# Conditioning weights of the first norm: multiplied on TensorE in column quarters instead of folded on VectorE

## The chip, the cores and the metric

The kernel runs on one core of a Trainium2 chip. The metric is the device time of one launch in microseconds (us). TensorE (PE in the profile; PEld is its weight load) multiplies, VectorE (DVE) and ScalarE (ACT) do elementwise work and reductions, GpSimd (POOL) does almost nothing here, and SyncE (SP) issues every DMA from one queue, in program order. Each engine runs its own instructions in order and waits for others by semaphores.

## The reference, cut to what matters

A two-layer trunk for 256 tokens of width 2048: in each layer a mixer and an MLP, each behind a norm whose shift and scale come from a conditioning vector `c`.

```python
cond = jax.nn.silu(c)                                  # [2048]
for l in range(2):
    mod = cond @ ada_w[l] + ada_b[l]                   # [2048] @ [2048, 6*2048]
    sh1, sc1, g1, sh2, sc2, g2 = split(mod, 6)
    h = rms_norm(x, norm1_g[l]) * (1 + sc1) + sh1      # the change is in this sh1, sc1 of l = 0
    y = mixer(h)
    x = x + g1 * y
    h = rms_norm(x, norm2_g[l]) * (1 + sc2) + sh2
    x = x + g2 * square(relu(h @ mlp_w1[l])) @ mlp_w2[l]
```

Nothing of the first layer can be multiplied before `sh1` and `sc1` of its columns are known: they need 2 x 2048 columns of `ada_w[0]`, 2048 rows each, or 64 DMAs of 512 KB.

## The kernel before, in words

Activations are held feature-major: a k-tile is 128 features by 256 tokens, and there are 16. Shift and scale of two k-tiles are made together, as a *pair* `pr` (0 to 7). For a pair, `load_ar` brings 4 tiles `ar`, each with 4 row blocks of `ada_w` by 512 columns (256 of shift, 256 of scale), in two DMAs; the ring has 4 such tiles, so the whole ring is one pair. `cond_sum` multiplies the 16 row blocks by their column of `cond` and adds them up on VectorE (L575 once, L577 15 times) into `acc`, 128 partitions by 512. `cond_pair` then sums over the partitions: `row_sums` transposes `acc` in four pieces (L317), ScalarE adds up each row (L320), and two small VectorE instructions give shift and scale (L588, L590), with which ScalarE makes the normed input `hf` of the two k-tiles (L595).

Around this the first products are laid out so that they can begin with few k-tiles. I call them phase 1 (k-tiles 0 to 3: values of six heads and first queries, `nb` and `q0b`, weights loaded in L624), phase 2 (k-tiles 0 to 7: gates and last values, `gbs` and `vbs`, weights from `wplain`, L607) and phase 3 (all k-tiles: other queries and keys, `qk`). In phase 3 the k-tiles 0 to 5 are multiplied as plain f32 (`hf` by `raw`), and from k-tile 6 on the weights are split into a high part (`wh`, ScalarE, L224) and a low part (`wl`, VectorE, L225). All these matmuls are issued by the helper `mm`, L124. The pairs 0 and 1 stand in phase 1, the sums of 2 and 3 with the first loads of phase 2, those of 4 and 5 in its second half, 6 and 7 in phase 3. `gates()` stands at k-tile 8 of phase 3 and needs all 16 k-tiles.

The eight banks of PSUM are handed out as four of `lin` (L) and four of `mix` (M0 to M3). In the three phases only M3 is free for the conditioning work. The order of each engine's instructions is set by a scheduler at build time, from the order of the code and its own estimates; it isn't changed at run time.

Of the kernel before, what the change touches and what calls it, by code (L numbers as in the profile page):

```python
# [9 lines left out]
F32 = mybir.dt.float32  # L10
# [3 lines left out]
OP = mybir.AluOpType  # L14
# [4 lines left out]
P = 128  # L19
# [7 lines left out]

# [1 line left out]
_C0 = {"ident": 128, "ones": 128}  # L29
# [58 lines left out]
def back(ap):  # L88
    """The same elements, last first along the free axis."""
    a = [list(s) for s in ap.ap]  # L90
    return bass.AP(tensor=ap.tensor, offset=ap.offset + a[1][1] - 1, ap=[a[0], [-1, a[1][1]]])
# [3 lines left out]
def tile_trunk(ctx: ExitStack, tc: tile.TileContext, io, out):  # L95
# [23 lines left out]
    def sums(n):  # L119
        """n banks for long sums: the four of `lin`, then the first of `mix`."""  # L120
        return [lbank() if i < 4 else bank(i - 4) for i in range(n)]
# [3 lines left out]

# [1 line left out]
    c0o, c0w = _cuts(_C0)  # L127
# [46 lines left out]

# [1 line left out]
    def newton(y, v, a):  # L176
        """y, near v ** -0.5, one step nearer."""
        V.tensor_tensor(a, y, y, op=OP.mult)
        V.scalar_tensor_tensor(a, a, -0.5, v, op0=OP.mult, op1=OP.mult)
        V.scalar_tensor_tensor(y, a, 1.5, y, op0=OP.add, op1=OP.mult)  # L180
# [11 lines left out]
    def spread(cols, which=None):  # L192
        """[128 tokens, 2] columns -> [128, 256] with the token on the free axis, on each partition."""
        dg = tmp.tile([P, T], F32, tag="diag", bufs=2, name="diag")
        for t in range(2):
            V.tensor_scalar(dg[:, t * P:(t + 1) * P], ident, cols[:, t:t + 1], None, op0=OP.mult)
        b = bank(which)
        mm(b[:, 0:T], ones, dg)
        return b[:, 0:T]
# [12 lines left out]
    def side():  # L212
        """The next of the small steps that go between the long products."""
        if pending:
            f = pending.pop(0)
            if f is not None:
                f()

# [1 line left out]
    def wsplit(raw, n):  # L220
# [7 lines left out]
    def wload(W, k0, kper, cols):  # L228
        """k-tiles k0.. of the column ranges `cols`, side by side, as exact high and low parts."""
        w = sum(c1 - c0_ for c0_, c1 in cols)  # L230
        raw = wp.tile([P, 1024], F32, tag="raw", bufs=4, name="raw")
        rv = raw[:, :kper * w].rearrange("p (k c) -> p k c", k=kper)
        o = 0
        for a, b in cols:
            SP.dma_start(rv[:, :, o:o + b - a],  # L235
                         W[k0 * P:(k0 + kper) * P, a:b].rearrange("(k p) c -> p k c", p=P))
            o += b - a
        return wsplit(raw, kper * w)

    def tmul(o, h, wh, wl, c, m, start, stop):  # L240
        """o[:, :256] + o[:, 256:] += W[:, c:c+m]^T h, feature-major."""
        mm(o[0:m, 0:2 * T], wh[:, c:c + m], h[:, 0:2 * T], start=start, stop=False)
        mm(o[0:m, 0:T], wl[:, c:c + m], h[:, 0:T], start=False, stop=stop)

    def linear(W, nk, kper, cols, hget, plan, evac, banks, stag=1, fill=None, k1=0):
        """Feature-major products. plan: one entry per bank, of one tile (offset in the W tile, width), whose
        product is the sum of the bank's halves, or of two tiles, one in each half."""
        w = sum(b - a for a, b in cols)
# [35 lines left out]
    def linear_n(W, nk, kper, c0_, hget, evac, fill=None, k1=0):  # L284
        """Token-major products of 512 columns."""
        bs = [lbank() for _ in range(2)]
        for k0 in range(k1, nk, kper):
            wh, wl = wload(W, k0, kper, [(c0_, c0_ + 512)])
            if fill is not None:
                fill()  # L290
            for t in range(2):
                for kk in range(kper):
                    k = k0 + kk
                    nmul(bs[t], hget(k), t, wh[:, kk * 512:(kk + 1) * 512], wl[:, kk * 512:(kk + 1) * 512],
                         k == k1, k == nk - 1)
                side()
        for t in range(2):
            evac(t, bs[t])
# [12 lines left out]

# [1 line left out]
    def row_sums(dst, tiles, func=AF.Copy, which=None):  # L313
        """dst[:, i] = the sum over the partitions of each column of func(tiles[i])."""
        b = bank(which)
        for i, t in enumerate(tiles):
            PE.transpose(b[:, i * P:(i + 1) * P], t, ident)  # L317
        for i in range(len(tiles)):
            j = tmp.tile([P, P], F32, tag="junk", bufs=2, name="junk")
            S.activation(j, b[:, i * P:(i + 1) * P], func, accum_out=dst[:, i:i + 1])  # L320
# [40 lines left out]
    class Fill:  # L361
        """Spreads the conditioning products over the weight tiles of a phase."""

# [21 lines left out]

# [1 line left out]
    class Norm:  # L387
# [43 lines left out]
    def residual(W, nk, hget, gate, norm, groups, stag, fill, done=None):  # L431
        """xT += gate * (W^T h); groups: the plans of output tiles that are held together, and their banks."""
        k0 = 0
# [56 lines left out]

# [1 line left out]
    wE = io["even_w_in"][0]  # L492
# [8 lines left out]
    def vtile():  # L501
        """Values of two heads, each with a column of ones behind."""
        v = vp.tile([P, 2, 2, 260], F32, tag="v", name="v")
# [10 lines left out]
    with ExitStack() as es:  # L514
# [9 lines left out]
        for t in range(2):  # L524
            for q in range(2):
                SP.dma_start(xn[t][q], x[t * P:(t + 1) * P, q * 1024:(q + 1) * 1024])
            if t == 0:
                SP.dma_start(c0, io["c0"])
                r0, n0 = load_rows(0)

        def load_ar(pr, kq):
            ar = sp0.tile([P, 4, 2, T], F32, tag="ar", bufs=4, name="ar")
# [8 lines left out]
        put_rows(0, r0, n0)  # L541
        S.activation(cond, prm[:, 96:112], AF.Silu)
        for i in (1, 2):
            put_rows(i, *rows[i - 1])
# [22 lines left out]
        def cond_sum(pr):  # L567
            """The products for the k-tiles 2 pr and 2 pr + 1, still to be summed over the partitions."""
            acc = sums_of[pr] = sp0.tile([P, 2, T], F32, tag="acc0", bufs=3, name="acc0")
            for kq in range(4):  # L570
                ar = early.pop(0) if early else load_ar(pr, kq)
                for kr in range(4):
                    cc = cond[:, kq * 4 + kr:kq * 4 + kr + 1]
                    if kq == 0 and kr == 0:
                        V.tensor_scalar(acc, ar[:, kr], cc, None, op0=OP.mult)  # L575
                    else:
                        V.scalar_tensor_tensor(acc, ar[:, kr], cc, acc, op0=OP.mult, op1=OP.add)  # L577

        def cond_pair(pr):
            """Shift, scale and the normed input of the k-tiles 2 pr and 2 pr + 1."""  # L580
            if pr not in sums_of:
                cond_sum(pr)
            acc = sums_of.pop(pr)
            cs = st(4, "adac")
            row_sums(cs, [acc[:, i // 2, (i % 2) * P:(i % 2 + 1) * P] for i in range(4)])
            two_k = slice(2 * pr, 2 * pr + 2)
# [12 lines left out]

        # The values of the first six heads and the first queries, over a quarter of the k-tiles, as these come.  # L600
        HALF = KT // 2
# [36 lines left out]

        # The gates of the first four heads and the values of the last two, over half of the k-tiles.
        gbs = [lbank() for _ in range(4)]  # L640
# [39 lines left out]
        def gates():  # L680
            """Weights of the scores of the first four heads, and the floors of their denominators."""
            gb = small.tile([8, 1], F32, tag="gb", bufs=1, name="gb")
# [57 lines left out]

        # The other queries and all keys of the first half of the heads, over all k-tiles.
        qk = sums(7)
# [25 lines left out]

# [1 line left out]
    mp = mixs.enter_context(tc.tile_pool(name="mp", bufs=1))  # L770
# [7 lines left out]
    def mix_head(hd, qt, kt, v, gate, weight, ml):  # L778
        """One head: masked, weighted scores, values, head norm, gate. v(t): the head's values of a token tile."""
        x_ = {}  # L780
# [125 lines left out]
    def segment(*units, k1=0):  # L906
        """256 feature-major columns for each (first column, what to do with their bank)."""
        n = len(units)
# [25 lines left out]

    # The rest of the first products.
    nb = sums(6)
# [64 lines left out]

# [1 line left out]
    fill = Fill([(1, 2)], 60)  # L1003
    hs = nrm.finish(1, 0)
    wO = io["odd_w_in"][0]
    with ExitStack() as es:
# [82 lines left out]

        # top 64 of the causal keys, as an additive mask  # L1090
        m8 = ap.tile([P, 8], F32, name="m8")
# [96 lines left out]

# [1 line left out]
    ready = set()  # L1190
# [47 lines left out]
```

## Time and profile before

| | |
|---|---|
| median of 3 runs | 2418.57 us (2410.31 to 2423.73) |
| profiled execution, span | 2418.6 us |
| TensorE, mean granted clock | 0.988 |
| busy: PE, DVE, ACT | 96%, 72%, 50% of the span |
| HBM read | 607.37 MB |

The profiled execution's span and the median of the runs agree within 0.1 us, so a sum made on the trace can be read against the median. A record's time includes the tail in which its result comes out, so that in a dense stream the next record starts before the last has ended; how fast matmuls go is read from the distance of their starts, or from the chain's rows, which give the time from the first start to the next piece.

### The profile page before, as it was taken

What the parts mean: (1) busy time and instruction counts of PE and PEld (TensorE: products, weight loads), DVE (VectorE), ACT (ScalarE), POOL (GpSimd) and SP (SyncE); (2) the same over time, 40 slices, a digit from 0 to 9 for tenths busy, and PEclk for the clock granted to TensorE, in tenths of its full rate; (3) what the DMA queues carried; (4) which work ended last, traced back from release to release, by engine and by line L of the source; (5) the groups of instructions that cost most, each with busy time, mean ns of one, the idle gap of its engine ahead of it and who ended that gap; (6) DMA issues with size and microseconds to landing.
All of it is one profiled execution on the core that took longest, in us unless ns stands there. A gap on an engine that the chain in (4) does not pass through costs nothing.

```text
span 2418.6 us, 38953 instructions
## 1 busy us (share of the span) xinstructions
PE 2331.7 (96%) x14877; PEld 2091.8 (86%) x14877; DVE 1737.4 (72%) x2555; ACT 1209.8 (50%) x2293; POOL 0.5 (0%) x8
## 2 busy tenths in 40 slices
PE   5899999999899999999999899999999999999999
PEld 3688889998788888899899799998888888999998
DVE  5768899987877777887877879886555546556554
ACT  2235554544555555655544445655555556444443
POOL 0000000000000000000000000000000000000000
PEclk9999999999899999999999999999999999999999
DMA  9998899988788898888888776675666666555653
GB/s 324 358 297 292 284 302 320 328 283 288 234 312 312 289 317 303 288 308 290 289 312 288 234 264 206 212 241 161 186 189 184 188 186 184 190 184 183 201 184 130
DMA packets 268911, 612.06 MB, mean 253 GB/s; under 512 B 26690, under 2 KB 95284, under 8 KB 268724
## 3 DMA queue, kind: packets, MB, share of 16 engines
q1 hardware_dynamic: 268724, 609.58, 76.2%
q8 instruction: 116, 1.90, 0.3%
q14 instruction: 71, 0.58, 0.1%
HBM read 607.37 MB, written 2.12 MB: 252 GB/s over the span
## 4 chain that ended last, share of the span: by engine, by line
PE 75%; DMA 9%; DVE 9%; issue 3%; ACT 2%; SPq 1%; DVEq 0%; ACTq 0%
PE L L124 45%; PE M L124 29%; DMA ada<-in_ada_w_dram 8%; DVE wl L225 3%; DVE acc L356 1%; DVE acc L577 1%; PE M L317 1%; DMA raw<-in_even_w_in_dram 1%; ACT wh L224 1%; SPq L235 0%; ACT junk L320 0%; DVE xT L441 0%; DVE cv L887 0%; DMA xn<-in_x_dram 0%; PE M L560 0%
## 5 line engine op out<-in xcount | busy, mean ns | idle before, releaser
L124 PE MATMUL L<-hs,wh 128*128 128x256 f32 (+1 forms) x5184 | 1362.2, 336 | 16.5 <-ACT hs L425 7.7
L224 ACT CAST wh<-raw 128x1024 fp32r<-128x1024 f32 (+2 forms) x736 | 765.0, 1042 | 872.5 <-PE M L124 465.9
L225 DVE TENSOR_TENSOR wl<-raw,wh 128x1024 fp32r<-128x1024 f32 (+2 forms) x736 | 888.0, 1212 | 426.5 <-ACT wh L224 425.6
L124 PE MATMUL L<-hs,wl 128*128 128x256 f32 x3696 | 1047.4, 284 | 7.0 <-DVE wl L225 6.9
L124 PEld LDWEIGHTS L<-hs,wh 128*128 128x128 f32 x5184 | 886.0, 192 | 112.6 <-ACT hs L425 8.1
L124 PE MATMUL M<-hs,wh 128*128 128x512 f32 (+1 forms) x2584 | 732.3, 347 | 0.0
L124 PEld LDWEIGHTS L<-hs,wl 128*128 128x128 f32 x3696 | 707.4, 192 | 9.7 <-DVE wl L225 8.3
L124 PE MATMUL M<-hs,wl 128*128 128x256 f32 x1988 | 561.8, 283 | 0.0
L124 PEld LDWEIGHTS M<-hs,wh 128*128 128x128 f32 x2584 | 446.0, 189 | 79.2 <-issue 1.6
L356 DVE SCALAR_TENSOR_TENSOR acc<-ada,cond,acc 128x1024 f32<-128x1024 f32 x300 | 384.9, 1283 | 141.1 <-DMA ada<-in_ada_w_dram 139.7
L124 PEld LDWEIGHTS M<-hs,wl 128*128 128x128 f32 x1988 | 377.5, 190 | 1.1 <-issue 0.3
L207 DVE TENSOR_TENSOR hs<-z,hs 128x256 fp32r<-128x256 f32 x256 | 105.7, 419 | 2.0 <-ACT hs L206 2.0
L320 ACT ACTIVATE junk<-M 128x128 f32<-128x128 f32 x226 | 59.4, 279 | 95.1 <-PE M L317 94.8
L206 ACT CAST hs<-z 128x256 fp32r<-128x256 f32 x256 | 101.5, 400 | 8.6 <-PE L L124 8.5
L577 DVE SCALAR_TENSOR_TENSOR acc<-ar,cond,acc 128x512 f32<-128x512 f32 x120 | 90.2, 751 | 5.6 <-DMA ar<-in_ada_w_dram 2.0
L481 ACT ACTIVATE half<-half 128x256 f32<-128x256 f32 x128 | 50.9, 412 | 48.1 <-DVE half L310 47.9
L124 PE MATMUL L<-hf,raw 128*128 128x256 f32 x224 | 53.6, 394 | 4.0 <-DMA raw<-in_even_w_in_dram 4.0
L124 PEld LDWEIGHTS L<-hf,raw 128*128 128x128 f32 x224 | 44.3, 199 | 13.0 <-issue 6.8
L317 PE MATMUL M<-c,acc 128*128 128x128 f32 x192 | 32.7, 297 | 21.5 <-DVE acc L577 7.8
L482 ACT ACTIVATE z<-half 128x256 f32<-128x256 f32 x128 | 50.9, 412 | 0.6
L317 PEld LDWEIGHTS M<-c,acc 128*128 128x128 f32 x192 | 23.5, 150 | 28.0 <-ACT junk L320 8.6
L320 ACT ACTIVATION_READ_ACCUMULATOR junk<-M 128x1 f32 x226 | 47.3, 209 | 0.0
(243 smaller groups left out, 1080.8 us busy)
## 6 DMA issues: line engine op xcount, KB each, us to landing
raw<-in_mlp_w_dram SPq DMA_DIRECT2D x512, 512.0 KB, 4.5
ada<-in_ada_w_dram SPq DMA_DIRECT2D x320, 512.0 KB, 6.0
raw<-in_even_w_in_dram SPq DMA_DIRECT2D x136, 256.0 KB, 5.5
ar<-in_ada_w_dram SPq DMA_DIRECT2D x64, 512.0 KB, 8.1
raw<-in_odd_w_in_dram SPq DMA_DIRECT2D x48, 512.0 KB, 4.5
raw<-in_even_w_out_dram SPq DMA_DIRECT2D x32, 512.0 KB, 6.1
raw<-in_odd_w_out_dram SPq DMA_DIRECT2D x32, 512.0 KB, 4.8
raw<-in_even_w_in_dram SPq DMA_DIRECT2D x28, 512.0 KB, 6.4
```

The costliest lines, as they stand in the source:

```text
L124: PE.matmul(o, a, b, start=start, stop=stop, skip_group_check=True)
L206: S.copy(h[:, 0:T], src)
L207: V.tensor_tensor(h[:, T:2 * T], src, h[:, 0:T].bitcast(F32), op=OP.subtract)
L224: S.copy(wh[:, :n], raw[:, :n])
L225: V.tensor_tensor(wl[:, :n], raw[:, :n], wh[:, :n].bitcast(F32), op=OP.subtract)
L317: PE.transpose(b[:, i * P:(i + 1) * P], t, ident)
L320: S.activation(j, b[:, i * P:(i + 1) * P], func, accum_out=dst[:, i:i + 1])
L356: V.scalar_tensor_tensor(acc, r, cond[:, kr:kr + 1], acc, op0=OP.mult, op1=OP.add)
L481: S.activation(a, a, AF.Relu)
L482: S.activation(zt, a, AF.Square)
L577: V.scalar_tensor_tensor(acc, ar[:, kr], cc, acc, op0=OP.mult, op1=OP.add)
```

## The change

Four edits belong together; the rest of the diff takes comments out, by which line numbers move by 7 behind the start.

```diff
+        quad = st(1, "nv")
+
+        def cond32(k):
+
+            return bass.AP(tensor=cond.tensor, offset=cond.offset + k, ap=[list(cond.ap[0]), [0, 32]])
...
         S.activation(cond, prm[:, 96:112], AF.Silu)
+        V.reduce_sum(quad, c0[:, 0:128:32], axis=AX.X)
...
         def cond_sum(pr):
-            acc = sums_of[pr] = sp0.tile([P, 2, T], F32, tag="acc0", bufs=3, name="acc0")
+            b = bank(3)
             for kq in range(4):
                 ar = early.pop(0) if early else load_ar(pr, kq)
                 for kr in range(4):
-                    cc = cond[:, kq * 4 + kr:kq * 4 + kr + 1]
-                    if kq == 0 and kr == 0:
-                        V.tensor_scalar(acc, ar[:, kr], cc, None, op0=OP.mult)
-                    else:
-                        V.scalar_tensor_tensor(acc, ar[:, kr], cc, acc, op0=OP.mult, op1=OP.add)
+                    mm(b[32 * kr:32 * kr + 32, :], cond32(kq * 4 + kr), ar[:, kr].rearrange("p c t -> p (c t)"),
+                       kq == 0, kq == 3)
+            acc = sums_of[pr] = sp0.tile([P, 2, T], F32, tag="acc0", bufs=3, name="acc0")
+            S.copy(acc.rearrange("p c t -> p (c t)"), b)
...
             acc = sums_of.pop(pr)
-            cs = st(4, "adac")
-            row_sums(cs, [acc[:, i // 2, (i % 2) * P:(i % 2 + 1) * P] for i in range(4)])
+            cs = bank(3)[:, 0:4]
+            for i in range(4):
+                mm(cs[:, i:i + 1], acc[:, i // 2, (i % 2) * P:(i % 2 + 1) * P], quad, i == 0, i == 3)
```

The 16 row blocks of a pair become 16 plain f32 matmuls. The stationary operand is one column of `cond`, repeated 32 times, so a product fills 32 partitions with the same row of 512 sums; the block `kr` of each `ar` writes to the quarter `32 kr` of bank M3, and the four `ar` of a pair are added up there. ScalarE copies the bank to `acc`. `quad` is 1 on the partitions 0, 32, 64 and 96 and 0 elsewhere, so a matmul of a quarter of `acc` by `quad`, with one column, adds the four quarters and turns the row into a column at once; it takes the place of the transposes and of the row sums.

TensorE's order at the second pair, where phase 1 goes from k-tile 1 to k-tile 2. `M_331` and, after the change, `M_296` and `M_327` are all bank M3; `M_223` to `M_225` and `M_225` to `M_227` are M0 to M2. Before:

```order
L317 MATMUL M_331<-c_78,acc_301 128x128 x4
L124 MATMUL L<-raw,hf 128x512 x4
L124 MATMUL M_223<-raw,hf 128x512
L124 MATMUL M_224<-raw,hf 128x512
L124 MATMUL M_225<-hf,raw 128x256 x2
```

Now:

```order
L124 MATMUL M_296<-ar,cond 32x512 x16
L124 MATMUL M_327<-nv,acc_325 128x1 x4
L124 MATMUL L<-raw,hf 128x512 x4
L124 MATMUL M_225<-raw,hf 128x512
L124 MATMUL M_226<-raw,hf 128x512
L124 MATMUL M_227<-hf,raw 128x256 x2
```

The 16 products stand in TensorE's queue ahead of the phase's next k-tiles, where only four transposes stood.

TensorE's order in the first k-tiles of phase 2, where pairs 2 (`M_391`) and 3 (`M_430`) are multiplied. Before:

```order
L124 MATMUL L<-hf,raw 128x256 x8
L124 MATMUL M_393<-raw,hf 128x512
L124 MATMUL M_394<-raw,hf 128x512
L124 MATMUL L<-hf,raw 128x256 x8
L124 MATMUL M_393<-raw,hf 128x512
L124 MATMUL M_394<-raw,hf 128x512
L317 MATMUL M_490<-c_78,acc_403 128x128 x4
```

Now:

```order
L124 MATMUL M_391<-ar,cond 32x512 x4
L124 MATMUL L<-hf,raw 128x256 x3
L124 MATMUL M_391<-ar,cond 32x512 x4
L124 MATMUL L<-hf,raw 128x256 x5
L124 MATMUL M_391<-ar,cond 32x512 x4
L124 MATMUL M_381<-raw,hf 128x512
L124 MATMUL M_382<-raw,hf 128x512
L124 MATMUL L<-hf,raw 128x256
L124 MATMUL M_391<-ar,cond 32x512 x4
L124 MATMUL L<-hf,raw 128x256 x7
```

Pairs 2 and 3 go between the phase's own products in groups of four, one group for each `ar`; the pairs 1, 4, 5, 6 and 7 stand as 16 in a row.

SyncE's queue from the loads of phase 3 on: the two runs of 8 `ar` are pairs 6 and 7, L235 loads the split weights. Before:

```order
L607 DMA raw<-in_even_w_in_dram 128x896 x12
L534 DMA ar<-in_ada_w_dram 128x4x256 x8
L235 DMA raw<-in_even_w_in_dram 128x896 x2
L534 DMA ar<-in_ada_w_dram 128x4x256
L235 DMA raw<-in_even_w_in_dram 128x896
L534 DMA ar<-in_ada_w_dram 128x4x256
L235 DMA raw<-in_even_w_in_dram 128x896
L534 DMA ar<-in_ada_w_dram 128x4x256 x6
```

Now:

```order
L614 DMA raw<-in_even_w_in_dram 128x896 x12
L540 DMA ar<-in_ada_w_dram 128x4x256 x8
L235 DMA raw<-in_even_w_in_dram 128x896 x3
L755 DMA c_661<-const_c_dram 128x896
L235 DMA raw<-in_even_w_in_dram 128x896
L690 DMA gb<-in_even_gate_b_dram 8x1
L693 DMA wg<-in_even_w_in_dram 128x16x8
L235 DMA raw<-in_even_w_in_dram 128x896 x3
L540 DMA ar<-in_ada_w_dram 128x4x256 x8
```

Up to the 12 loads of phase 3 the queue is the same as before; behind them seven loads of split weights now stand ahead of pair 7, where four stood.

## Rows read from the trace of the kernel before

**Rows 1.** The page: busy time of each engine over the whole span.

```profile
PE 2331.7 (96%) x14877; PEld 2091.8 (86%) x14877; DVE 1737.4 (72%) x2555; ACT 1209.8 (50%) x2293; POOL 0.5 (0%) x8
```

**Rows 2.** Stretches: start:end, length, busy PE PEld DVE ACT POOL, PEclk, DMA, GB/s.

```profile
34.35:65.19 30.84, 28.58 (x69) 14.22 (x70) 21.98 (x34) 7.38 (x21) 0.00 (x0) 0.94 1.07 366
65.19:110.60 45.41, 42.87 (x173) 31.33 (x171) 31.92 (x50) 9.54 (x31) 0.00 (x0) 1.00 1.04 347
110.60:164.80 54.20, 50.16 (x261) 44.83 (x260) 37.87 (x62) 12.56 (x42) 0.00 (x0) 0.94 0.96 314
...
205.00:330.00 125.00, 122.05 (x746) 108.94 (x746) 108.11 (x147) 68.03 (x111) 0.10 (x1) 1.00 0.89 289
```

**Rows 3.** What reads the `ar` tiles: count, min/median/max ns, first and last start.

```profile
L577 DVE SCALAR_TENSOR_TENSOR acc<-ar,cond,acc x120: 741/752/753, 17.6 to 165.1; 128x512 f32<-128x512 f32 x120
L575 DVE TENSOR_SCALAR acc<-ar,cond x8: 479/484/487, 14.6 to 151.7; 128x512 f32<-128x512 f32 x8
DMA to landing us min/median/max: 3.8/8.1/10.6
```

**Rows 4.** The chain from 30 to 155 us: start, us to the next piece, what.

```profile
34.35 5.56 PE L L124 x8
...
51.20 5.40 PE L L124 x8
56.60 2.58 PE M L124 x8
59.18 3.43 PE L L124 x8
...
70.36 3.45 PE L L124 x16
73.82 1.72 PE M L124 x4
...
114.60 6.38 PE L L124 x16
120.98 2.59 PE M L124 x12
...
154.67 1.92 PE L L124 x17
```

**Rows 5.** PE's waits from 26 to 172 us: total, times, longest.

```profile
PE M L317 <- DVE acc L577: 7.8, 3, 4.0
PE L L124 <- ACT hf L595: 4.5, 2, 2.3
PE L L124 <- DMA raw<-in_even_w_in_dram: 4.0, 1, 4.0
```

**Rows 6.** The timeline of the start; L534 issues the last two `ar` of pair 0.

```profile
17.08 2.04 SPq L534 DMA_DIRECT2D ar<-in_ada_w_dram  x4
24.66 6.26 DVE L577 SCALAR_TENSOR_TENSOR acc<-ar,cond,acc 128x512 f32<-128x512 f32 x8
```

**Rows 7.** PE's timeline at the half-row products of layer 1.

```profile
1417.14 0.28 PE L124 MATMUL L<-hs,wl 128*128 128x256 f32 x1
1417.35 0.92 PE L124 MATMUL M<-ik,iq 64*128 64x256 f32 x8
```

**Rows 8.** The timeline: narrow sums on PE, a copy of a bank on ACT.

```profile
185.47 0.72 PE L124 MATMUL M<-lfc,c 128*128 128x4 f32 x6
65.23 0.58 ACT L637 COPY q<-M 128x512 f32<-128x512 f32 x1 [0.28 <-PE M L124]
```

**Rows 9.** PE's timeline at pair 7 and the gates behind it.

```profile
165.97 0.63 PE L317 MATMUL M<-c,acc 128*128 128x128 f32 x4 [1.24 <-DVE acc L577]
167.15 1.54 PE L124 MATMUL L<-hs,wh 128*128 128x256 f32 x8 [0.56 <-ACT wh L224]
...
169.13 0.63 PE L124 MATMUL M<-hs,wh 128*8 128x512 f32 x1
...
171.50 0.40 PE L124 MATMUL M<-hs,wh 128*8 128x512 f32 x1
```

## Prediction

> **What bounds the kernel now.** I read the page's busy times first: TensorE is busy 96% of the span and VectorE 72% [rows 1], so work that goes from one to the other goes to the scarcer engine, unless TensorE waits where it lands. The fold ends near 165.1 + 0.75 = 166 us [rows 3], so the next view is the busy time by stretch up to 330 us [rows 2]. To see there: from its first product at 34.35 us to 164.8 us TensorE is busy 92 to 95% of each stretch, and from 205 us on 122.05 of 125.00 us. So a delay of TensorE behind the phases is a delay of the end, and a gain there is a gain of the end. The DMA engines are full until about 110 us (share 1.07 and 1.04) [rows 2], so neither the fold nor TensorE alone sets the pace there.
>
> The chain gives TensorE's own price [rows 4]. The program's four 128x512 f32 products into L appear as 8 records, that is two for each product, and they take 3.43 us: 0.429 us a record. A k-tile of phase 1 takes 3.43 + 2.58 = 6.01 us, of phase 2 3.45 + 1.72 = 5.17, of the f32 part of phase 3 3.45 + 2.59 = 6.04. With 4, 8 and 6 k-tiles the phases are 24.0, 41.4 and 36.2 us of issue.
>
> [...] At pair 7 stand waits of 1.24 and 0.56 us, and the clock is low again: a gate record takes 0.63 us at 169.13 and 0.40 at 171.50 [rows 9]. From 167.15 to about 171.06, where the records change, are 3.9 us; at 0.40 to 0.63 they cost 1.4 too much, at half the clock 1.95; I take 1.7. [...]
>
> **The change part by part.**
>
> *The fold leaves VectorE.* 120 x 0.752 + 8 x 0.484 = 94 us of it [rows 3]. [...]
>
> *The products come to TensorE.* A pair has 16 products, by the same two records each 32 of 0.429 us. One after another they take 13.7 us; four at once, 3.43. No row of before has a product in a column quarter. The nearest is the pair of half-row products in layer 1 [rows 7]: 8 records, four of 256 columns and four of 128, which one after another need 4 x 0.215 + 4 x 0.107 = 1.29 us and the tail of 0.17, 1.46 in all; they took 0.92, and halves that run side by side throughout would take 0.65 + 0.17 = 0.82. So two products in separate halves do run side by side, in spite of two records each. I take four at once, 3.43 us, since that is the nearest row, and keep 13.7 as the other bound. The same rows show what it costs to go in: the half-row product starts 0.21 us behind the last whole one, whose 256 columns take about 0.11. I assume the same on the way out, 0.2 us together. Pairs 2 and 3 stand in groups of four between other products, so pairs 1 to 7 have 1 + 4 + 4 + 4 = 13 such places: 2.6 us.
>
> [...]
>
> *The sum over partitions.* Four matmuls of one column with a whole 128x128 stationary: 8 records. The nearest row, 6 records with four columns, takes 0.72 us with its tail [rows 8], so some 0.095 each behind it, 0.95 us for the eight with tail. They replace four transposes. On the way of a pair's shift and scale, a ScalarE copy of 0.58 us [rows 8] replaces ScalarE's four row sums.
>
> *The start.* The last `ar` of pair 0 is issued at 17.08 + 2.04 = 19.1 us [rows 6]; a median of 8.1 us to landing [rows 3] gives 27 us, and it had landed by 24.66 + 4 x 0.78 = 27.8 us, when the fold came to it without a wait. Behind it come one group of four (0.86 us warm, 1.7 at the low clock, and the tail), the copy 0.6, the sum 1.2, two small VectorE steps 0.35 and `hf` 0.65: first product at 31.7 us instead of 34.35.
>
> *The phases after.* Phase 1: 24.0, the low clock 2.1, pair 1 with 3.6, then 2.8 us until `hf` stands (tail, copy, sum, two steps, `hf`), and the low clock again, 2.0: 34.5, to 66.2 us; before, 65.19. Phase 2: 41.4 + four pairs 13.7 + ten changes 2.0 + two sums 1.9 + 0.3 waiting = 59.3, to 125.5 us. Before, it ended at 110.6 and phase 3 began at 114.60. The weights of phase 3 are there by then, since they landed at 114.5 us before, so the wait and the low clock fall away: 36.2 + two sums 1.9 = 38.1, to 163.6 us, against 154.67 before. Then pair 6 (3.6), k-tiles 6 and 7 (10.1, as from 154.67 to 164.80 before), pair 7 (3.6), two sums (1.9) and the records that stood from 167.15 to 171.06, at full clock (3.9 − 1.7 = 2.2): 21.4, to 185.0 us. Before, this place was 171.06. It is 13.9 us later.
>
> What hides nothing: the ring of `ar` is now freed by TensorE, but by the sums above it frees those of pair 4 between 108 and 112 us, and pair 5 is needed from 122 us on; its 8 x 0.52 MB at 347 GB/s [rows 2] take 12 us, so a microsecond of waiting is possible there. Pair 6 stands in TensorE's queue ahead of k-tile 6, and whatever it waits for, the split products wait too; behind pair 5 and the 12 weights of 0.46 MB it has landed near 150 us and is needed at 164. Nothing behind the gates changes but by the shift.
>
> **Sum:** 2418.6 + 13.9 = 2432.5, or 2433 us, 0.6% slower.
>
> **The rivals.**
>
> *One after another* (or only part side by side). If quarters don't overlap, each of seven pairs costs 10.3 us more: 2433 + 72 = 2505. If two at a time, 3.4 more: 2433 + 24 = 2457. For it: no column quarter in the trace. Against: the side-by-side halves [rows 7].
>
> *The waits swallow it* (not slower). TensorE's queue would then have no low clock and no wait left from phase 1 on: with the last `ar` at 25 us it starts at 30 us, and the rest is 24.0 + 41.4 + 36.2 + 12.3 of old work, 7 x 3.43 of products and 7 x 0.95 of sums: 174.6 us, 3.5 later, so 2422. It decides where TensorE waits for `hf` of pair 1 less than half a microsecond and keeps its clock from the first product on. For it: the waits are there, 16.3 us [rows 5]. Against: at pair 1 nothing else stands in the queue between product, copy, sum and `hf`, so a wait like that of 2.3 us stays.
>
> *Faster through VectorE.* 94 us of a busy engine are free. Against: TensorE lacks only 2.95 us in 205 to 330 us [rows 2], so with the case above it gives 2422 − 3 = 2419; to be faster by more, the products must cost less than a quarter of what their records say, for instance one record each: 12 us less, 2407.
>
> *Hidden anyway:* the change moves no bound, 2419. Against: the 92 to 95% [rows 2].
>
> **How the numbers follow.** Runs of this kernel differ by 13 us, so 0.5%, 12 us, is about what can be told from no change. Chances: four at once as summed 0.60, with its own range 2425 to 2443; two at a time 0.10; one after another 0.12; the waits swallow it or hidden 0.10; faster 0.08. Of the first, three in five lie above 2430.7. Slower by over 0.5%: 0.36 + 0.10 + 0.12 = 0.58; within: 0.24 + 0.10 = 0.34; faster 0.08. The range leaves out one after another and faster, 0.20: 2414 to 2462.
>
> **What the profile of the changed kernel would show.** Products `ar,cond` 32x512: 256 records whose starts stand by fours; busy time of all near 8 x 3.5 = 28 us, and not 110. First phase-1 product at 31 to 32 us. Phase 3 begins near 125 us with no wait for weights, and no wait of DVE at pair 7; the gates at 185 us. Everything behind shifted alike. I would be wrong if the records of a pair span 7 or 14 us, if the start comes no earlier, or if the stretch beyond 185 us has another length than before.

## The result and the profile after

The changed kernel takes 2433.65 us (median of 5 runs, 2427.53 to 2438.28), the kernel before 2416.71 beside it (5 runs, 2408.6 to 2423.73): a ratio of 1.0067, 95% interval 1.0045 to 1.0089. It is slower by 0.7%; the forecast was 2433 us, 0.6% slower. By the medians the loss is 16.9 us. The profiled span is 2434.2 us against 2418.6, the granted clock 0.990 against 0.988, so the two traces differ by 15.6 us.

The page's busy times after, to set beside [rows 1]: VectorE lost 91.5 us of work, and TensorE gained 26.2.

```profile
PE 2357.9 (97%) x15165; PEld 2094.0 (86%) x15165; DVE 1645.9 (68%) x2428; ACT 1205.5 (50%) x2237; POOL 0.5 (0%) x8
```

Where the time went is read best from one stretch, from the first product of phase 1 to the first transposes of the heads' outputs (`yn`), since TensorE stands in one line there. Busy time by stretch (start:end, length, busy PE PEld DVE ACT POOL, PEclk, DMA, GB/s), first of the kernel before:

```profile
34.35:342.70 308.35, 292.94 (x1612) 243.35 (x1612) 242.63 (x384) 123.58 (x245) 0.10 (x1) 0.98 0.95 313
```

and after:

```profile
30.55:357.30 326.75, 318.38 (x1860) 249.09 (x1861) 163.44 (x272) 120.26 (x196) 0.11 (x1) 0.99 0.91 300
```

TensorE's busy time there grows by 25.4 us, its idle time (length less busy) falls from 15.4 to 8.4, and the stretch starts 3.8 us earlier: 25.4 − 7.0 − 3.8 = 14.6 us at the first `yn`. In these two executions only 1.0 us is added from there to the end.

The three phases after, the same view as [rows 2]:

```profile
30.55:63.18 32.63, 30.84 (x104) 14.49 (x104) 1.84 (x6) 6.83 (x14) 0.00 (x0) 0.95 1.08 364
63.18:123.21 60.03, 60.03 (x306) 34.57 (x305) 2.08 (x8) 9.24 (x18) 0.00 (x0) 1.00 0.89 300
123.21:176.23 53.02, 53.02 (x312) 45.64 (x309) 10.66 (x21) 11.89 (x22) 0.00 (x0) 1.00 0.95 306
```

In phases 2 and 3 TensorE has no idle time left up to pair 7, and none at pair 7 either, so it waits for no DMA there; VectorE stands nearly empty (2.08 us of 60.03 in phase 2). The fold's time on a free engine became issue time on the full one. PE's timeline after shows the pieces (start, us with the last one's tail, what; the idle time before it in brackets):

```profile
25.73 1.92 PE L124 MATMUL M<-ar,cond 128*32 128x512 f32 x16
28.36 1.05 PE L124 MATMUL M<-nv,acc 128*128 128x1 f32 x8 [0.70 <-ACT acc L583]
30.55 3.70 PE L124 MATMUL L<-raw,hf 128*128 128x512 f32 x8 [1.14 <-ACT hf L602]
...
42.78 3.64 PE L124 MATMUL M<-ar,cond 128*32 128x512 f32 x32
47.12 1.05 PE L124 MATMUL M<-nv,acc 128*128 128x1 f32 x8 [0.70 <-ACT acc L583]
49.26 5.40 PE L124 MATMUL L<-raw,hf 128*128 128x512 f32 x8 [1.08 <-ACT hf L602]
...
63.18 1.06 PE L124 MATMUL M<-ar,cond 128*32 128x512 f32 x8
64.18 1.56 PE L124 MATMUL L<-hf,raw 128*128 128x256 f32 x6
...
105.53 3.64 PE L124 MATMUL M<-ar,cond 128*32 128x512 f32 x32
109.10 3.72 PE L124 MATMUL L<-hf,raw 128*128 128x256 f32 x16
...
135.40 0.95 PE L124 MATMUL M<-nv,acc 128*128 128x1 f32 x8
136.21 3.70 PE L124 MATMUL L<-hf,raw 128*128 128x256 f32 x16
...
161.45 3.64 PE L124 MATMUL M<-ar,cond 128*32 128x512 f32 x32
...
176.23 3.64 PE L124 MATMUL M<-ar,cond 128*32 128x512 f32 x32
180.61 1.02 PE L124 MATMUL M<-nv,acc 128*128 128x1 f32 x8
181.93 0.39 PE L124 MATMUL M<-hs,wh 128*8 128x512 f32 x1
...
182.95 0.40 PE L124 MATMUL M<-hs,wh 128*8 128x512 f32 x1
```

The products as a group (count, busy time of all, mean ns of one, idle time before):

```profile
L124 PE MATMUL M<-ar,cond 128*32 128x512 f32 x256 | 31.8, 598 | 0.0
```

A pair's 32 records reach from 105.53 to the next piece at 109.10, 3.57 us; a group of 8 from 63.18 to 64.18, 1.00 us. One record is 0.598 us with its tail and would be 0.429 in a dense stream [rows 4]: eight of them one after another would take 3.4 us. So four products do run at once, in spite of two records each. What a change of width costs beside that is seen in the chain (start, us to the next piece; M takes together what goes to the `mix` banks, products, narrow sums and all):

```profile
90.56 4.59 PE M L124 x28
95.15 3.56 PE L L124 x16
98.71 1.72 PE M L124 x4
100.43 3.45 PE L L124 x16
103.88 5.29 PE M L124 x36
109.17 3.65 PE L L124 x16
...
126.93 2.59 PE M L124 x12
129.52 3.45 PE L L124 x16
132.97 3.38 PE M L124 x20
136.35 3.56 PE L L124 x16
```

Sixteen records into L take 3.45 us between their like, 3.56 behind a narrow sum and 3.65 behind a pair's products. So a place where quarters stand costs 0.14 us on the way in (1.00 − 8 x 0.429 / 4 = 0.14 for a group, 3.57 − 3.43 = 0.14 for a pair) and 0.20 on the way out, 0.34 in all. A narrow sum costs 3.38 − 2.59 = 0.79 and 0.11 on the way out, 0.90.

### The profile page after: what moved, and what is told of

It is laid out like the page before. It is cut to its first block, busy times and chain, and to the rows that moved or that the text cites. A ratio compares the mean times of both kernels' runs of the same rounds, so it can differ in the third digit from the quotient of the medians.

```text
span 2434.2 us, 39322 instructions
## 1 busy us (share of the span) xinstructions
PE 2357.9 (97%) x15165; PEld 2094.0 (86%) x15165; DVE 1645.9 (68%) x2428; ACT 1205.5 (50%) x2237; POOL 0.5 (0%) x8
## 4 chain that ended last, share of the span: by engine, by line
PE 80%; DMA 8%; DVE 8%; issue 2%; ACT 2%; SPq 1%; DVEq 0%; ACTq 0%
PE L L124 46%; PE M L124 32%; DMA ada<-in_ada_w_dram 7%; DVE wl L225 3%; DVE acc L356 1%; PE M L317 1%; ACT wh L224 1%; SPq L235 0%; DVE xT L441 0%; PE M L567 0%; ACT junk L320 0%; DVE sc L1105 0%; DMA raw<-in_even_w_in_dram 0%; DMA rows<-in_even_head_norm_g_dram 0%; DVE m L1104 0%
## 5 line engine op out<-in xcount | busy, mean ns | idle before, releaser
L320 ACT ACTIVATE junk<-M 128x128 f32<-128x128 f32 x194 | 51.0, 279 | 20.7 <-PE M L317 20.5
L124 PEld LDWEIGHTS L<-hf,raw 128*128 128x128 f32 x224 | 41.8, 190 | 13.3 <-issue 7.2
L124 PE MATMUL L<-wh,hs 128*128 128x512 f32 x128 | 42.0, 391 | 0.0
L320 ACT ACTIVATION_READ_ACCUMULATOR junk<-M 128x1 f32 x194 | 40.7, 210 | 0.0
```

Of the source, the lines that this page charges most:

```text
L124: PE.matmul(o, a, b, start=start, stop=stop, skip_group_check=True)
```

## The experiments

My theory, A, was the sum on record: the products run four at once, the pairs cost TensorE their issue time, and only part of it falls into waits that vanish. The rival B put the time down to something else than issue (the ring of `ar`, the queue). A third, C, was set up for the last two runs: half or more of the loss comes from the other order of instructions behind the gates. That the narrow sums are to blame is a rival as well; e2_sum_only and e8_products_only bear on it.

All runs, with the places of TensorE's line in each profiled execution. The ratio is to the runs of the kernel before that stand beside them (29 beside e1, e2, e3 and e5, median 2414.48; 13 beside e6 and e8, 2416.44; 5 beside after, 2416.71); busy and idle are TensorE's from its first product to the first `yn`, us.

| kernel | median, us | ratio [95%] | first product | last gate record | first `yn` | busy | idle |
|---|---|---|---|---|---|---|---|
| before | | 1 | 34.35 | 175.34 | 342.7 | 292.9 | 15.4 |
| e2_sum_only | 2417.19 | 1.0019 [1.0002, 1.0036] | 33.16 | 174.19 | 346.9 | 295.3 | 18.5 |
| e3_pair0 | 2419.85 | 1.0023 [1.0009, 1.0037] | 30.63 | 173.35 | 345.4 | 297.2 | 17.6 |
| e5_pairs045 | 2426.95 | 1.0048 [1.0026, 1.0070] | 31.08 | 180.57 | 351.6 | 305.1 | 15.4 |
| e6_not67 | 2430.76 | 1.0058 [1.0038, 1.0079] | 31.01 | 185.35 | 356.0 | 314.6 | 10.4 |
| after | 2433.65 | 1.0067 [1.0045, 1.0089] | 30.55 | 187.15 | 357.3 | 318.4 | 8.4 |
| e8_products_only | 2435.35 | 1.0077 [1.0056, 1.0098] | 32.31 | 192.32 | 363.9 | 319.8 | 11.8 |
| e1_full_width | 2513.34 | 1.0412 [1.0378, 1.0446] | 38.30 | 267.48 | 436.1 | 391.5 | 6.3 |

**Full width (e1_full_width).** The products keep their number, but each has 128 columns of the same `cond` instead of 32; all 16 go to the whole bank, and the sum takes one row.

```diff
-            ... ap=[list(cond.ap[0]), [0, 32]])
+            ... ap=[list(cond.ap[0]), [0, P]])
...
-        V.reduce_sum(quad, c0[:, 0:128:32], axis=AX.X)
+        V.tensor_copy(quad, c0[:, 0:1])
...
-                    mm(b[32 * kr:32 * kr + 32, :], ..., kq == 0, kq == 3)
+                    mm(b, ..., kq + kr == 0, kq + kr == 6)
```

> The changed kernel, but each of the 16 products of a pair has the whole width: the column of cond is repeated 128 times, all 16 are added up in all partitions of bank M3, and the last sum takes partition 0 alone. Same result, same DMAs, same number of records; only the quarters are gone. Theory A (the change costs what TensorE needs to issue the products, four side by side): a pair goes from 3.47 us to 32 x 0.429 = 13.7 us, seven pairs lie where TensorE is full, so 72 us more and 2 to 3 at the start: 2505 to 2510 us. Theory B (the cost of the change is not the products but the ring of ar and the changed queue of SyncE): the products are small against it, and the time stays below 2450 us.

It takes 2513.34 us, a little above what A expected, and 83 more than after by the ratios (1.0412 / 1.0067 = 1.0343). Its timeline at pair 5:

```profile
164.57 13.90 PE L124 MATMUL M<-ar,cond 128*128 128x512 f32 x32
178.30 3.62 PE L124 MATMUL L<-hf,raw 128*128 128x256 f32 x16
```

The pair takes 13.73 us to the next piece, 0.429 for each of its 32 records, so here they run one after another; the quarters take 3.57 us, 3.85 times faster, 96% of four times. Seven pairs at 13.73 − 3.57 = 10.2 us are 71 us, and TensorE's busy time grew by 73.2. The first product came 7.75 us later than after (38.30), where I had expected 2 to 3, since pair 0's last products took 10.46 us behind the late `ar`. B expected less than 2450 us and falls: the loads are the same in both, and the time follows the issue. That after the change no wait for a DMA is left on TensorE from pair 1 to the gates says the same of the quarters.

**The narrow sums alone (e2_sum_only)**, on the kernel before: the fold stays on VectorE.

```diff
-            cs = st(4, "adac")
-            row_sums(cs, [acc[:, i // 2, (i % 2) * P:(i % 2 + 1) * P] for i in range(4)])
+            cs = bank(3)[:, 0:4]
+            for i in range(4):
+                mm(cs[:, i:i + 1], acc[:, i // 2, (i % 2) * P:(i % 2 + 1) * P], one1, i == 0, i == 3)
```

> The kernel before with one part of the change: the fold stays on VectorE, but the sum over the partitions is four matmuls with a column of ones, read from the bank by VectorE, in place of transposes and ScalarE's row sums. Theory A: 8 records of about 0.1 us in place of 4 of 0.11 cost TensorE 0.4 us a pair, 3 us in all; each of the three places where TensorE waits for shift and scale (pairs 0, 1 and 7) gets 1.0 to 1.2 us shorter. Together -1 to +1 us, within 0.2% of before. Theory B says the same.

1.0019, against 1.0067: a little over a quarter of the change's loss, by the interval anything from none to half, so the narrow sums alone don't make the loss. PE's waits from 26 to 172 us (total, times, longest) say why the earlier `hf` gains nothing:

```profile
PE M L124 <- DVE acc L577: 12.0, 3, 4.6
PE L L124 <- ACT hf L596: 2.2, 2, 1.1
PE L L124 <- DMA raw<-in_even_w_in_dram: 1.0, 1, 1.0
```

Against [rows 5] the wait for `hf` falls from 4.5 to 2.2 us and that for weights from 4.0 to 1.0, and the wait for the fold rises from 7.8 to 12.0. The fold ends last there, and what TensorE saves it waits at the next pair.

**Pair 0 alone, and pairs 0, 4 and 5 (e3_pair0, e5_pairs045).** All pairs keep the narrow sums; those not in `TE` are folded on VectorE as before.

```diff
+        TE = (0,)            # e5_pairs045: (0, 4, 5); e6_not67: (0, 1, 2, 3, 4, 5)
         def cond_sum(pr):
+            if pr not in TE:
+                ...
+                            V.scalar_tensor_tensor(acc, ar[:, kr], cc, acc, op0=OP.mult, op1=OP.add)
+                return
...
-                mm(cs[:, i:i + 1], ..., quad, i == 0, i == 3)
+                mm(cs[:, i:i + 1], ..., quad if pr in TE else one1, i == 0, i == 3)
```

> Only pair 0 is multiplied on TensorE in quarters, pairs 1 to 7 are folded on VectorE; all pairs are summed by the narrow matmuls. Theory A: pair 0 lies where TensorE has nothing to do, so the first product comes at 30.5 us instead of 34.35 and TensorE gets no products where it is full; phase 3 still can't begin before its weights land, near 113 us, so of the 3.8 us at the start 1 to 3 are left: 2412 to 2417 us on the scale of a kernel before of 2417. Theory B: the ring is still freed by VectorE, like before: 2417 or a little less as well. Slower than before by over 0.3% would speak against both.

> Pairs 0, 4 and 5 on TensorE in quarters, pairs 1, 2, 3, 6 and 7 folded on VectorE. Theory A: the products of 4 and 5 (7 us) fill the time that TensorE waited for the weights of phase 3 (4.0 us, and 2.9 us of low clock behind it), so phase 3 begins near 114 us at full clock; VectorE reaches pairs 6 and 7 earlier, and the wait of 1.8 us at pair 7 gets shorter. 2407 to 2414 us, 0.1 to 0.4% faster than before. Theory B: with two pairs late in the ring freed by TensorE, a part of the loss of the changed kernel stays: 2420 us or more.

Both missed: 1.0023 and 1.0048 where I had hoped for less than before. PE's timeline of e3_pair0 where phase 3 begins:

```profile
112.72 3.69 PE L124 MATMUL L<-hf,raw 128*128 128x256 f32 x16 [0.89 <-DMA raw<-in_even_w_in_dram]
```

and of e5_pairs045:

```profile
101.59 3.64 PE L124 MATMUL M<-ar,cond 128*32 128x512 f32 x32
...
118.81 1.06 PE L124 MATMUL M<-ar,cond 128*32 128x512 f32 x8 [0.33 <-DMA ar<-in_ada_w_dram]
119.95 3.69 PE L124 MATMUL L<-hf,raw 128*128 128x256 f32 x16
```

I had meant to hide pairs 4 and 5 in the wait for phase 3's weights and its low clock, 6.9 us in the kernel before (4.0 of waiting [rows 5], and 6.38 − 3.45 = 2.9 for the 16 records behind it [rows 4], whose granted clock was 0.57). But in e3_pair0 that wait is only 0.89 us (in e2_sum_only 1.02), and its products run at 3.69, so there was nothing left to hide in: phase 3 begins 7.2 us later, and the last gate record stands at 180.57 against 173.35, 7.22 us for two pairs. That is 3.61 a pair, about the issue time. Theory A's price stands; my reading of what that wait was worth behind other edits failed.

The chain of the kernel before shows that the wait hung on the fold, too (start, us, what):

```profile
107.15 0.48 DVE acc L575
...
107.68 0.50 SPq L534
...
108.23 6.24 DMA raw<-in_even_w_in_dram
```

SyncE's queue has the weights behind the `ar` of pair 5, whose places in the ring the fold of pair 4 has to free; from 90 to 120 us the queue waits 8.8 us for L577 ahead of `ar` loads. The weights are issued from 108.23 us on, in e3_pair0 from 106.11 and in e2_sum_only from 105.10.

What e3_pair0 loses does not stand ahead of the gates: its last gate record is 2.0 us earlier than before, its first `yn` 2.7 us later. In e2_sum_only it is the same, 1.2 us earlier and 4.2 later. Why is open.

**All but pairs 6 and 7 (e6_not67).** With `TE` as in the diff above.

> The changed kernel, but pairs 6 and 7 are folded on VectorE, which has nothing else to do by then; pairs 0 to 5 stay on TensorE. Theory A (each pair costs TensorE what its products need, 3.56 us as the two kernels with one and with three pairs showed): 7.1 us of products leave TensorE behind phase 2, and a wait at pair 7 of some 3 us with the low clock behind it comes back. The gates come 2 to 5 us earlier than in the changed kernel, at 177 to 180 us, and the time is 2 to 5 us less: a ratio to before of 1.004 to 1.006. Theory C (half or more of the loss comes from the other order of instructions behind the gates, not from the products): the gates come earlier, but the time stays that of the changed kernel.

1.0058, as A has it, but the interval holds C's forecast, the 1.0067 of after, too; this run doesn't tell them apart. The first gate record comes at 177.85 us, 4.1 us earlier than after, the last only 1.8, not 7.2. What the two pairs cost is replaced by a wait and by slow gates, 0.63 us a record against 0.39; from PE's waits and its timeline:

```profile
PE M L124 <- DVE acc L586: 2.9, 1, 2.9
```

```profile
178.45 0.63 PE L124 MATMUL M<-hs,wh 128*8 128x512 f32 x1
```

**The products with the old sums (e8_products_only).** Four transposes and ScalarE's row sums come back, with 1/32 in the copy, since 32 partitions hold each sum.

```diff
-            S.copy(acc.rearrange("p c t -> p (c t)"), b)
+            S.activation(acc.rearrange("p c t -> p (c t)"), b, AF.Copy, scale=1.0 / 32.0)
...
-            cs = bank(3)[:, 0:4]
-            for i in range(4):
-                mm(cs[:, i:i + 1], ..., quad, i == 0, i == 3)
+            cs = st(4, "adac")
+            row_sums(cs, [acc[:, i // 2, (i % 2) * P:(i % 2 + 1) * P] for i in range(4)], which=3)
```

> The other half of the change alone: products in the quarters for all eight pairs, but the sum over the partitions by transposes and ScalarE's row sums as before (the copy of the bank multiplies by 1/32, since each sum stands 32 times in its quarter). Theory A: the narrow sums cost TensorE 0.4 us a pair more than the transposes and save 1.1 us at pairs 0 and 1, where TensorE waits; without them the gates come within 1.5 us of the changed kernel's 181.9 us, and the time is the same within 0.2%: a ratio to before of 1.005 to 1.008. Theory C, that the order behind the gates decides, would let it differ by more, either way.

The time is within what I expected, 1.0077, the gates are not: their first record stands at 187.09, 5.2 us later than after. PE's timeline at its first product, and its waits:

```profile
32.31 5.21 PE L124 MATMUL L<-raw,hf 128*128 128x512 f32 x8 [2.26 <-ACT hf L599]
```

```profile
PE L L124 <- ACT hf L599: 4.5, 2, 2.3
PE M L124 <- DMA ar<-in_ada_w_dram: 1.8, 1, 1.8
```

So the narrow sums shorten the way to `hf` (2.2 us of waits against 4.5). The rest of the 5.2 us is less clearly theirs: the two stretches behind these waits take 5.21 and 6.65 us against 3.70 and 5.40, with granted clocks of 0.70 and 0.55 against 1.00 and 0.68, and pair 7's last `ar` is 1.8 us late. The medians lie just 1.7 us apart, within the runs' scatter, so it isn't shown that the narrow sums pay, and not that they cost. In this execution the way from the first `yn` to the end is 6.9 us shorter than after (2070.0 against 2076.9); why is open.

**What the runs show together.** The delay of the first `yn` is about the loss of time: 4.2, 2.7, 8.9, 13.3, 14.6, 21.2 and 93.4 us, in the order of the table, against 4.6, 5.6, 11.6, 14.0, 16.2, 18.6 and 99.5 by the ratios (times 2415 us). A single trace is less sure than this looks: from the first `yn` to the end the eight profiled executions take from 2065.5 us (e2_sum_only) to 2076.9 (after), and that of e2_sum_only ends 6.2 us before the one of the kernel before, though its first `yn` is 4.2 us later. So differences of a few us go by the ratios. After the change 11.8 of the 14.6 us at the first `yn` are there at the last gate record already, so in these traces C, half or more from behind the gates, does not hold, though a part does lie there. None of the kernels beats the one before.

## Why the prediction was right

**The bound** was read rightly: time on TensorE in the phases is time at the end, and 91.5 us less of VectorE bought nothing but waits of TensorE.

**Four at once, 3.43 us a pair:** right; 3.57 with the way in, and 256 records whose busy time is 31.8 us in all (forecast 28, without the tails). *One after another* and *two at a time* are ruled out by these records and by e1_full_width, *faster* by the number of the records.

**The places where quarters stand:** 0.2 us each was too low. They cost 0.34, so 13 of them 4.4 us, not 2.6. It is part of why phase 2 took 60.03 us, and not 59.3.

**The narrow sum, 0.95:** measured 0.90 with the way out.

**The start, 31.7:** 30.55. The forecast took 27.8 us, where the fold came to the last `ar`, for its landing, and so had the last products end at 28.9. They ended at 25.73 + 1.92 = 27.65, without a wait for a DMA. The rest to the first product took 2.9 us; forecast 2.8.

**The low clock:** forecast twice in phase 1. The second came as said (5.40 us at 49.26 us, the same as before, granted clock 0.68), the first did not (3.70 us at 30.55, granted clock 1.00). With the start this makes phase 2 begin at 63.18 us and not at 66.2. No run shows the 2.1 us that the sum takes for the first as a price of the clock: it is 5.56 − 3.43 of the kernel before [rows 4], where the granted clock on record is 1.00; the 2.0 for the second is 5.40 − 3.43, at 0.68 in both kernels. Nor does one show the 1.7 us "at the low clock" for a group of four in the start: the last 16 records of pair 0 took 1.92 us, at a granted clock of 1.00. The waits for weights and for the fold at pair 7 are gone, as forecast, and the gates run at 0.39 us a record, with a granted clock of 1.00; of the kernel before's, those from 169.13 to 171.06 us had 0.50 (0.63 us a record [rows 9]). From 123.21 to 161.45 us, where pair 6 begins, are 38.2 us; forecast 38.1.

The place that was 171.06 us, the gates' fourth record, is at 182.95, 11.9 us later; forecast 13.9. In the chain of the kernel before four transposes take 0.44 us to the next piece:

```profile
141.70 0.44 PE M L317 x4
142.14 3.46 PE L L124 x16
```

So the terms, now with measured sizes, are: seven pairs of products 24.0, their places 4.4, seven narrow sums instead of transposes 7 x (0.90 − 0.44) = 3.2. That is 31.6 of issue. TensorE's busy time grew by only 25.4, 6.2 less, and what it had lost in slow stretches at the start, at 114.60 us and at pair 7 and lost no more is as much: (5.56 − 3.70) + (6.38 − 3.45) + 1.7 = 6.5, of which the 1.7 is the prediction's estimate.

**"Nothing behind the gates changes but by the shift"** was the step that failed. The last gate record is 11.8 us late, the first `yn` 14.6, and the end 15.6. PE's waits from 182 to 365 us after:

```profile
PE L L124 <- DVE v L509: 4.1, 2, 3.8
PE M L709 <- ACT gl L704: 1.3, 1, 1.3
```

Before, these two were 2.1 and 0.3 us:

```profile
PE L L124 <- DVE v L509: 2.1, 2, 1.8
PE M L702 <- ACT gl L697: 0.3, 1, 0.3
```

The two errors, 2.0 too much ahead of the gates and 3.7 too little behind them, nearly cancel; the hit on the total is better than its parts. It owes something to luck as well: the forecast added 13.9 us to 2418.6, while the kernel before took 2416.71 beside the changed one and the loss by the medians is 16.9. The times of the gates and of the first `yn` are each from one execution. As far as they go, the loss behind the gates isn't tied to the products: from the last gate record to the first `yn` are 167.4 us before, 170.2 after, 168.6 in e1_full_width, and 170.7 to 172.7 in the other variants, the most in e2_sum_only, which has none on TensorE. The order of VectorE's and ScalarE's instructions there is set anew in each build; whether it makes `v` and `gl` late was not isolated and stays open.

**The waits swallow it** came half true: idle time fell by 7.0 us, the slow stretches by 6.5, and 31.6 us of issue are more than both and the 3.8 us at the start together.

## What to carry to other kernels

Price moved work on the engine that is full, stretch by stretch, and credit only the waits that still stand once the other edits are made: of the 6.9 us in front of phase 3 only 1.0 was left as soon as the sums alone were changed. Freeing a busy engine that isn't last gained nothing here but the waits for it: 91.5 us less of VectorE, 7.0 less of TensorE's idle time. Follow one landmark through all variants (here the first head's transposes): it shows where a delay arises. Whether it reaches the end is told by the medians of many runs.

## What the runs showed of the hardware

Column quarters of plain f32 ran side by side, with two records a product: 3.57 us a pair against 13.73 at full width. The way in and out of them cost 0.14 and 0.20 us, 0.34 together.

The slow first stretch of phase 1 isn't always the clock that the records show. Stretches of the kernel before, at the first product and at the next k-tiles' first:

```profile
34.35:39.91 5.56, 5.56 (x9) 2.54 (x10) 4.61 (x8) 1.04 (x3) 0.00 (x0) 1.00 1.09 348
51.20:56.60 5.40, 5.40 (x9) 2.39 (x10) 2.02 (x5) 1.04 (x3) 0.00 (x0) 0.68 1.09 349
```

The second has a granted clock of 0.68; the first is as slow with 1.00 on record, and the prediction took both for the clock. In e3_pair0 the first stretch took 6.73 us with 0.54 on record, behind the same pair 0 and the same wait for `hf` (1.15 us) as after, where it took 3.70 with 1.00. What decides it there stays open; it is worth 2 to 3 us between executions of nearly the same start.
